# A fused transformer layer in fp32: four places where an in-order engine holds back TensorE are reordered or given buffers

## The chip, the cores and the metric

One Trainium2 chip, one of its cores. The metric is the time of one execution in device microseconds (us), without a profiler; three runs of the kernel before were timed. One further execution was taken with the hardware profiler, and all rows below come from it. Its time is compared with the runs in the section on the profile.

A core has TensorE (PE in the profile; PEld is its weight load), VectorE (DVE), ScalarE (ACT), GpSimd (POOL), and SyncE (SP), which here only issues transfers (DMA). Each of the engines works through one list of instructions in the order in which the program was built.

## The reference

One step of a small encoder layer for 1024 prompt rows and 8 x 16 sample rows (1152 rows, width 1024):

```
h   = RMSNorm(x)
z   = h @ W_in          # FoX q,k,v,logits | GDN q,k,v,a,b | GDN out gate gg | merge gates A,B
yA  = P_fox(FoX(h))     # causal attention with forget weights, 8 heads of 64
yB  = P_gdn(rmsnorm(GDN(h)) * silu(gg))   # gated delta rule, 8 heads of 64, chunks of 64 rows
x  += RMSNorm(W_out(sigmoid(gA) * yA + sigmoid(gB) * yB))
x  += RMSNorm(W_down relu(W_up RMSNorm(x))^2)      # 1024 -> 4096 -> 1024
```

It returns the new rows, and also FoX's keys and values, the logits, the GDN state and the last rows of the convolution. The GDN part solves one 64 x 64 triangular system for each chunk and head.

## The kernel before

All products are made in fp32 accuracy by splitting each operand into a high and a low part (`split`: a cast on ACT, L356, and a subtraction on DVE, L357) and adding three products (`mm3`, L157). Activations are kept transposed; a row block is `CH` = 384 columns, so that a product of 128 output features with 1152 rows is three chains of 24 matmuls, one for each `c`.

A scheduler of the framework orders the instructions of each engine at build time. It takes what is ready by its own estimate of durations, by priorities in the code: `tc.high_priority(n)` raises (or lowers) the priority of what stands under it, and `tc.issue_after(ins)` forbids it to be issued ahead of another instruction. On the chip the orders are fixed, and an engine whose next instruction isn't ready waits. A tile with `bufs=n` in a pool gets its memory in turn from n buffers under one tag; the next user waits until the last reader of that buffer is done, a DMA that stores it included.

The stages, with their place in the profiled execution:

- 0 to 50 us: RMSNorm of the rows, transposed by `to_T` (L195 casts the high part on ACT), and the first products. `early_parts` (L259) casts the weights of two small products.
- 50 to 660: the delta rule for four pairs of heads, p = 0 to 3. For each: `gdn_in` (products; ACT copies their banks to `X`, L428), `gdn_norms` (convolution on DVE, L478 to L482; Silu on ACT, L483), `gdn_systems` (decays: Exp on ACT, L543), `gdn_inverse` (30 steps of two DVE instructions, L592 and L593, a round trip through DRAM, a transposition, L609), `gdn_b` (states and outputs `oT`). At the end of `gdn_b` stands the gate: for each c, load `gg`, Silu on ACT (L702), two loads of row factors, a product on POOL (L704), and a product into `oT` on DVE (L705, "STT" below). The next pair's projections run beside it. The tiles `ro` and `gg` share three buffers of tag `be`.
- Into all of this, and into the next stage, the scheduler puts "fills": products of h with the weights for FoX, the out gate and the merge gates, at the lowest priority (`fill`, L407). They use two PSUM banks of tag `mf`; ACT copies each bank to a tile `gst` (L221) and sends it to DRAM (L222).
- 660 to 950: FoX. For a pair of heads `fox_prep` transposes v (two blocks of 512 columns and one of 128), then k alike. Each block is copied from its bank by ACT to a tile `kst` (L957, L969; v's last block goes to `vn`) and stored to the output by SP. `kst` has one buffer: every copy waits for the store ahead of it. For p = 1 to 3 this runs inside FoX, ahead of the pair that needs it.
- 950 to 1075: the merge: casts of `oparts` (`ohi<-orw`), Sigmoids of the gates `ga`, products, their sum. It may only start after the last fill (`issue_after(last_fill.ins)`). Then the output product, to 1200, and the up phase, to 1545.
- 1546 to 1895: the down phase, a fast matrix product of 7 passes `PASS = (1, 2, 3, 5, 6, 7, 4)`, each with 16 steps into four banks. The operands are split four steps ahead (`AHEAD`). At a pass's end `end(m, t, acc)` empties its four banks, for m = 2, 6 and 7 by additions on DVE (L1747 for m = 2). Six such banks and a bank for sums are there.

Of the kernel before, what the change touches and what calls it, by code (L numbers as in the profile page):

```python
# [72 lines left out]
def tile_step(ctx, tc, x_prompt, x_sample, cache_k, cache_v, cache_logf, state_gdn, state_conv,  # L73
# [140 lines left out]
    todo += [((W_MA, W_MB)[i] + j * P, gate_d[i, j]) for j in range(KT) for i in range(2)]  # L214

    def spill_out(pool, tag, bufs, w0, dst, c, acc):
        g = pool.tile([P, CH], F32, tag=tag, bufs=bufs, name=nm("gst"))
        if w0 < W_FK:
            A.activation(g, acc, AF.Copy, scale=-0.125)
        else:  # L220
            A.copy(g, acc)  # L221
        A.dma_start(dst[:, c * CH:(c + 1) * CH], g)  # L222
# [6 lines left out]
    with tc.tile_pool(name="p0", bufs=1) as p0:  # L229
# [60 lines left out]
        for t in range(NTT):  # L290
            xt = xts[t] if t < 6 else p0.tile([P, D], F32, tag="xt", bufs=6, name=nm("xt"))
            if t > 2:
                S.dma_start(xt, xp[t * P:(t + 1) * P] if t < 8 else xs)
            hns[t] = p0.tile([P, D], F32, tag="nh", name=nm("nh"), bufs=3)

            with tc.issue_after((nh if t < 3 else hh).ins) if t else ExitStack():
                nh = norm(xt, gb, p0, hns[t])
            if t == 0:
                raws = early_weights()
            if t == 2:  # L300
                with tc.issue_after(nh.ins):
                    logits_weights(raws)
                    for u in range(3):
                        if u == 2:
                            with tc.issue_after(hh.ins):
                                early_parts(raws)
                        hh = to_T(hns[u], u, hhi, hlo)
            elif t > 2:
                to_T(hns[t], t, hhi, hlo)
            if t % 3 == 2:  # L310
                logits_mm(t // 3)
                early_mm(t // 3)
            if t == 5:
# [94 lines left out]
    def fill():  # L408

        with tc.high_priority(-LOW):  # L410
            for w0, dst in todo[NE:]:
                mm = spill(w0, dst, "f", "mf", 20, MFB)
        return mm

# [98 lines left out]
    def gdn_systems(gp, p, qs, ks, vs, nv, kn, rows_n):  # L513
# [23 lines left out]
        d3 = u3(dk)  # L537
        G.tensor_tensor(d3, u3(gcb), bc(cols[:, 0], 2, [P, NU, C]), ALU.subtract)
        for u in (slice(0, NUP // 2), slice(NUP // 2, NUP)):
            V.tensor_tensor(d3[:, u], d3[:, u], bc(madd, 1, [P, NUP // 2, C]), ALU.add)  # L540
        V.tensor_tensor(d3[:, NUP:], d3[:, NUP:], bc(madds, 1, [P, NU - NUP, C]), ALU.add)
        A.activation(dk, dk, AF.Exp)
        A.activation(gcb, gcb, AF.Exp)  # L543
        gam = big(gp, "gam", 2, [P, NUP + NB])
# [38 lines left out]
        return kT, vs, qa, cols, gam, nv, kn, obd, sy  # L583

    def gdn_inverse(gp, obd, sy):


        st = big(gp, "st", 1, [4 * NU, 256])
        for k in range(1, 31):
            n = 31 - k  # L590
            tv = st[:, :k * n].rearrange("p (j i) -> p j i", j=k)
            V.tensor_tensor(tv, bc(sy[:, 0:k, k], 2, [4 * NU, k, n]), bc(sy[:, k, k + 1:], 1, [4 * NU, k, n]), ALU.mult)  # L592
            V.tensor_tensor(sy[:, 0:k, k + 1:], sy[:, 0:k, k + 1:], tv, ALU.subtract)  # L593
        V.memset(sy.rearrange("p j i -> p (j i)")[:, 0:1024:33], -1.0)
# [6 lines left out]
        for h in range(2):  # L601
# [5 lines left out]
            for q in range(2):  # L607
                S.dma_start(pk[r0:r0 + 64, q], inv_d[2 * h + q, 0:NUP].rearrange("(t u) j i -> (u j) t i", u=2))
        V.transpose(pk[:, 2].rearrange("p t i -> p (t i)"), pk[:, 0].rearrange("p t i -> p (t i)"))  # L609
        m2 = pt("pa", 1)  # L610
# [17 lines left out]
    def gdn_b(gp, p, kT, vs, qa, cols, gam, nv, kn, tt):  # L628
# [68 lines left out]
        to_rows(gp, nv[:, 1, :18], 18, rows_o.rearrange("h (t p) -> (h t) p", p=P), "pd", "rsbb")  # L697
        for c in range(3):
            cs = slice(c * CH, (c + 1) * CH)
            ro, gg = big(gp, "be", 3, [P, 512])[:, :CH], big(gp, "be", 3, [P, 512])[:, :CH]  # L700
            S.dma_start(gg, gg_d[p, :, cs])
            A.activation(gg, gg, AF.Silu)  # L702
            rows_bc(ro, rows_o[:, cs])
            G.tensor_tensor(gg, gg, ro, ALU.mult)  # L704
            V.scalar_tensor_tensor(oT[:, cs], oT[:, cs], ngc, gg, ALU.mult, ALU.mult)  # L705
        S.dma_start(gdn_d[p], oT)
        S.dma_start(gdn_p[0, 0, 2 * p:2 * p + 2].rearrange("h k v -> (h k) v"), st_)

    def to_rows(gp, src, n, dst, tag="pa", stag="rsb"):
# [232 lines left out]

    def fox_prep(fp, p, *banks):

# [3 lines left out]
        for src, i, dp, ds in ((v, 2, fv_p, fv_s), (k, 1, fk_p, fk_s)):  # L948
            S.dma_start(src, fr_d[i, p])
            for g in range(3):  # L950
                n = 4 if g < 2 else 1
                tp = banks[g % 2]() if banks else alt("pb", "pd")
                for j in range(n):
                    T.transpose(tp[:, j * P:(j + 1) * P], src[:, (4 * g + j) * P:(4 * g + j + 1) * P], ident)
                if g < 2:
                    st = fp.tile([P, 4, P], F32, tag="kst", bufs=1, name=nm("kst"))
                    A.copy(st.rearrange("p a n -> p (a n)"), tp)  # L957
                    S.dma_start(dp[0, 0, g * 512:(g + 1) * 512, 2 * p:2 * p + 2].rearrange(
                        "(a t) h d -> t a (h d)", a=4), st)
                    if src is v:  # L960
                        blk = v2[:, 4 * g:4 * g + 4].rearrange("p t (a d) -> p t a d", a=4)
                        sv = st.rearrange("p t (a d) -> p t a d", a=2)
                        A.copy(blk[:, :, 0:4:3], sv)
                        V.tensor_tensor(blk[:, :, 1:3], sv, f(blk[:, :, 0:4:3]), ALU.subtract)
                else:
                    st = vn
                    if src is k:
                        st = fp.tile([P, 4, P], F32, tag="kst", bufs=1, name=nm("kst"))[:, 0]
                    A.copy(st, tp[:, :P])  # L969
                    S.dma_start(ds[0][:, :, 2 * p:2 * p + 2].rearrange("b t h d -> (b t) (h d)"), st)  # L970
# [7 lines left out]
    with tc.tile_pool(name="gp", bufs=1, reuse_waits="tile") as gp:  # L978
# [6 lines left out]
        for kd in kds:  # L985
            G.memset(kd, 0.0)
        last_fill = fill()
        nxt = gdn_norms(gp, 0, *gdn_in(gp, 0, lg))
        cur = None
        for p in range(NG):  # L990
# [4 lines left out]
            with tc.high_priority(IOFF):  # L995
                tt = gdn_inverse(gp, *cur[7:])
            prev = *cur[:7], tt
            if p == 0:
# [16 lines left out]
            with tc.high_priority(BOFF):  # L1015
                gdn_b(gp, p, *prev)

# [135 lines left out]
    with tc.tile_pool(name="fp", bufs=1, reuse_waits="tile") as fp:  # L1153
# [17 lines left out]
        for p in range(NP_):  # L1171
            q, k, v2, vn, qkn = nxt
            oT = fp.tile([P, NPR], F32, tag="oT", bufs=2, name=nm("oT"))
            for hh in range(2):
# [12 lines left out]
                for s in (3, 2, 1, 0) if (p, hh) == (3, 1) else range(4):  # L1187
                    pr = fox_scores(fp, s, *qk)
                    if p + hh + s == 0:
                        first = tre[0]  # L1190
                    if late:
                        values(*late)
                    late = p, hh, s, pr, v2, oT
                    for sm in sms:
                        next(sm, None)
                    if hh and p < 3 and s == 1:
                        nxt = fox_prep(fpa, p + 1)
        values(*late)
# [34 lines left out]
    with tc.tile_pool(name="op", bufs=1, reuse_waits="tile") as op:  # L1233
# [28 lines left out]
        with tc.high_priority(200):  # L1262
# [6 lines left out]
            for c in (1, 0):  # L1269
                for k in range(4):  # L1270
                    load(1, k, c)
        def merge_weights(j):
# [3 lines left out]
        for j in range(KT):  # L1276
# [7 lines left out]
            for c, i in [(c, i) for i in (1, 0) for c in (2, 1, 0)] if j == 0 else [(c, i) for c in range(3) for i in (1, 0)]:  # L1284
# [5 lines left out]
                with tc.high_priority(200):  # L1290
                    if j == 0 and i:
                        ga = gas_[c]
                        with tc.issue_after(sp_.ins):
                            A.activation(ga, ga, AF.Sigmoid)
# [448 lines left out]
    def end(m, t, acc):  # L1743
        if m == 1:
            A.copy(yb[t][:, L], acc)
        elif m == 2:
            V.tensor_tensor(ya[t][:, L], acc, yb[t][:, L], ALU.add)  # L1747
        elif m == 3:
# [3 lines left out]
        elif m == 6:  # L1752
            V.tensor_tensor(yb[t][:, L], acc, yb[t][:, L], ALU.add)
            V.tensor_tensor(ya[t][:, R], ya[t][:, R], yb[t][:, R], ALU.add)
            V.tensor_tensor(ya[t][:, R], ya[t][:, R], yb[t][:, L], ALU.add)
        elif m == 7:
            V.tensor_tensor(yb[t][:, L], acc, yb[t][:, L], ALU.add)
            V.tensor_tensor(yb[t][:, R], yb[t][:, R], yb[t][:, L], ALU.add)
        else:
            y, (xt, ss) = yb[t], last[t]  # L1760
            with tc.high_priority(200):
# [9 lines left out]
                y_rows(xt, 4 + t, R)  # L1771

    def terms(hs, ls):

        return [(hs[0], ls[0]), (hs[0], ls[1]), (hs[1], ls[0])]

    for m in PASS:
# [59 lines left out]
```

## Time and profile before

| | |
|---|---|
| timed runs | 1892.69, 1892.87, 1893.63 us; median 1892.87 |
| profiled execution | 1903.8 us, span 1902.1 |
| PE busy | 1856.8 us, 98% of the span |
| DVE, ACT, POOL busy | 67%, 54%, 11% |

The profiled execution took 10.9 us more than the median. PE was idle for 1902.1 - 1856.8 = 45.3 us of its span; this counts only time in which no matmul ran, not time in which matmuls ran at a lower clock. A share of 98% says little on where time goes; the places where PE waited are in the view of waits, and the times at a lower clock in the windows, which have a granted clock for each stretch.

### The profile page before, as it was taken

The page shows a single profiled execution, that of the slowest core. Times are in us where ns is not written, and L with a number is a line of the kernel's source. Part 1 is how long each engine was busy: PE and PEld are TensorE (multiplying, and loading weights), DVE is VectorE, ACT ScalarE, POOL GpSimd, SP SyncE. Part 2 cuts the span into 40 slices and gives each one's busy share as a digit, 9 for nine tenths or more (in the row PEclk, how much of TensorE's full clock was granted, in tenths as well). Part 3 has the DMA queues.
Part 4 walks back from the last instruction along what each step waited for, and adds up shares of the span by engine and source line. Part 5 has one row for each costly group of instructions (what it writes and reads, how often), then busy time and mean ns, then how long its engine had stood idle before and what let it go on. Part 6 is the DMA issues. An engine that isn't in the chain of part 4 may idle for free. (4 is left out here: it accounts for less than half of the span.)

```text
span 1902.1 us, 31953 instructions
## 1 busy us (share of the span) xinstructions
PE 1856.8 (98%) x11035; PEld 1684.2 (89%) x11035; DVE 1270.7 (67%) x3096; ACT 1019.6 (54%) x2381; POOL 204.9 (11%) x340
## 2 busy tenths in 40 slices
PE   7999999999999999999999999999999999999998
PEld 6989989898898988888889988999999998788886
DVE  7458477686764385777555466977776664659697
ACT  6353574764847474666454454554555554345453
POOL 1221232322412100000012100000000000000000
PEclk9999999999999998999999999999999999999999
DMA  7133323233354353543355641244444478846473
GB/s 211 38 95 84 90 74 103 55 92 104 75 141 137 115 159 114 150 114 101 95 183 158 193 154 65 61 134 136 146 136 132 131 234 287 276 135 179 151 265 133
DMA packets 291155, 258.49 MB, mean 136 GB/s; under 512 B 68620, under 2 KB 245948, under 8 KB 290993
## 3 DMA queue, kind: packets, MB, share of 16 engines
q1 hardware_dynamic: 250629, 221.98, 39.7%
q10 hardware_dynamic: 40364, 34.47, 5.5%
q8 instruction: 87, 1.43, 0.3%
q14 instruction: 75, 0.61, 0.1%
HBM read 183.66 MB, written 72.71 MB: 135 GB/s over the span
## 5 line engine op out<-in xcount | busy, mean ns | idle before, releaser
L157 PE MATMUL mf<-hhi,whi 128*128 128x384 f32 x744 | 261.5, 351 | 2.5 <-ACT gst L221 2.4
L157 PE MATMUL mf<-hlo,whi 128*128 128x384 f32 x744 | 261.9, 352 | 0.0
L157 PE MATMUL mf<-hhi,wlo 128*128 128x384 f32 x744 | 261.6, 352 | 0.0
L157 PE MATMUL mm<-th,wh 128*128 128x320 f32 (+1 forms) x896 | 177.9, 295 | 0.0
L157 PE MATMUL mm<-bh,ah 128*128 128x512 f32 x436 | 169.7, 389 | 1.5 <-DVE y L1747 1.5
L157 PE MATMUL mm<-bl,ah 128*128 128x512 f32 x436 | 169.7, 389 | 0.0
L157 PE MATMUL mm<-bh,al 128*128 128x512 f32 x436 | 169.7, 389 | 0.0
L356 ACT CAST ah<-ar 128x512 fp32r<-128x512 f32 x107 | 66.4, 622 | 153.6 <-PE mm L157 101.6
L157 PEld LDWEIGHTS mf<-hhi,whi 128*128 128x128 f32 x744 | 141.0, 190 | 4.0 <-ACT gst L221 3.3
L157 PEld LDWEIGHTS mm<-th,wh 128*128 128x128 f32 x896 | 143.0, 188 | 0.0
L157 PEld LDWEIGHTS mf<-hhi,wlo 128*128 128x128 f32 x744 | 141.1, 190 | 0.7
L157 PEld LDWEIGHTS mf<-hlo,whi 128*128 128x128 f32 x744 | 141.0, 189 | 0.8
L157 PE MATMUL mm<-th,wl 128*128 128x256 f32 x448 | 131.4, 293 | 0.0
L1511 DVE TENSOR_TENSOR s<-mm,s 128x256 f32<-128x256 f32 (+1 forms) x196 | 84.3, 454 | 66.9 <-PE mm L157 53.8
L357 DVE TENSOR_TENSOR al<-ar,ah 128x512 fp32r<-128x512 f32 x107 | 73.7, 689 | 75.6 <-ACT ah L356 74.0
L357 DVE TENSOR_TENSOR wlo<-raw,whi 128x512 fp32r<-128x512 f32 x110 | 80.1, 730 | 49.0 <-ACT whi L356 43.9
L157 PE MATMUL mm<-hhi,whi 128*128 128x384 f32 x288 | 105.6, 367 | 4.3 <-ACT X L428 4.2
L356 ACT CAST whi<-raw 128x512 fp32r<-128x512 f32 x110 | 67.8, 619 | 70.1 <-PE mm L157 32.8
L157 PE MATMUL mm<-hhi,wlo 128*128 128x384 f32 x288 | 99.5, 346 | 0.0
L157 PE MATMUL mm<-hlo,whi 128*128 128x384 f32 x288 | 99.2, 345 | 0.0
L157 PE MATMUL mm<-mhi,wh 128*128 128x256 f32 (+1 forms) x336 | 99.1, 295 | 0.0
L157 PE MATMUL mm<-mlo,wh 128*128 128x256 f32 (+1 forms) x336 | 98.9, 294 | 0.0
(550 smaller groups left out, 4914.9 us busy)
## 6 DMA issues: line engine op xcount, KB each, us to landing
ar<-ua_d SPq DMA_DIRECT2D x124, 256.0 KB
raw<-in_w_in_dram SPq DMA_DIRECT2D x86, 256.0 KB
br<-in_w_down_dram SPq DMA_DIRECT2D x78, 256.0 KB
wr<-in_w_up_dram SPq DMA_DIRECT2D x56, 256.0 KB
ua_d<-s SPq DMA_DIRECT2D x112, 128.0 KB
ua_d<-s ACTq DMA_DIRECT2D x84, 128.0 KB
gate_d<-gst ACTq DMA_DIRECT2D x48, 192.0 KB
ga<-gate_d SPq DMA_DIRECT2D x48, 192.0 KB
```

The costliest lines, as they stand in the source:

```text
L157: mm = T.matmul(out, a, b, start=first and i == 0, stop=last and i == n - 1)
L356: a = A.copy(h, raw)
L357: V.tensor_tensor(l, raw, f(h), ALU.subtract)
L1511: V.tensor_tensor(r, o, x, ALU.add)
```

## The change

It has five parts. No matmul is added or taken away.

1. **Start.** The casts of `early_parts` come behind all three `to_T`, and no longer between the second and the third.
2. **Gates.** `gdn_b` returns the gate as a function; it is called after `gdn_inverse` of the next pair, and its three products on DVE may be issued only behind that inverse's steps 24, 28 and its transposition (called 31). The last pair's gate stays where it was. In `gdn_systems` a subtraction on POOL (1152 columns) is cut in two, and two Exp on ACT in two halves each: 4 instructions more on POOL and 8 on ACT.
3. **Keys and values.** Where `fox_prep` runs inside FoX (p = 1 to 3), `kst` has three buffers.
4. **Merge.** The splits of the GDN operands for c = 1 and 0 may be issued only behind the copies of the third-last and the second-last bank of the fills, the first three Sigmoids only behind the last copy. Before, these Sigmoids were issued after the splits for c = 2.
5. **Down phase.** In the last step of a pass the operands of a coming step are made after the banks are emptied (for m = 2, 6, 7 behind the last addition), and the second additions for m = 6 and 7 follow after all four first ones.

```diff
@@ spill_out
-            A.copy(g, acc)
+            gsts.append(A.copy(g, acc))
@@ start
                     for u in range(3):
-                        if u == 2:
-                            with tc.issue_after(hh.ins):
-                                early_parts(raws)
                         hh = to_T(hns[u], u, hhi, hlo)
+                    with tc.issue_after(hh.ins):
+                        early_parts(raws)
@@ fill
-        return mm
+        return mm, gsts[-3:]
@@ gdn_systems
-        G.tensor_tensor(d3, u3(gcb), bc(cols[:, 0], 2, [P, NU, C]), ALU.subtract)
+        for u in (slice(0, NUP // 2), slice(NUP // 2, NU)):
+            G.tensor_tensor(d3[:, u], u3(gcb)[:, u], bc(cols[:, 0, u], 2, [P, u.stop - u.start, C]), ALU.subtract)
...
-        A.activation(dk, dk, AF.Exp)
-        A.activation(gcb, gcb, AF.Exp)
+        for x in (dk, gcb):
+            for c in HALF:
+                A.activation(x[:, c], x[:, c], AF.Exp)
@@ gdn_inverse
-            V.tensor_tensor(sy[:, 0:k, k + 1:], sy[:, 0:k, k + 1:], tv, ALU.subtract)
+            steps[k] = V.tensor_tensor(sy[:, 0:k, k + 1:], sy[:, 0:k, k + 1:], tv, ALU.subtract)
...
-        V.transpose(pk[:, 2]...)
+        steps[31] = V.transpose(pk[:, 2]...)
@@ gdn_b (the loop over c is unchanged but for the issue_after)
+        def gate(behind=()):
+            for c in range(3):
...
+                with tc.issue_after(behind[c].ins) if behind else ExitStack():
+                    V.scalar_tensor_tensor(oT[:, cs], oT[:, cs], ngc, gg, ALU.mult, ALU.mult)
+            S.dma_start(gdn_d[p], oT)
...
+        return gate
@@ the loop over pairs, after gdn_inverse
+            if p:
+                with tc.high_priority(BOFF):
+                    gate([steps[k] for k in (24, 28, 31)])
...
-                gdn_b(gp, p, *prev)
+                gate = gdn_b(gp, p, *prev)
+                if p == NG - 1:
+                    gate()
@@ FoX
-                        nxt = fox_prep(fpa, p + 1)
+                        nxt = fox_prep(fpa, p + 1, kst=lambda _: fp.tile([P, 4, P], F32, tag="kst", bufs=3, name=nm("kst")))
@@ merge
             for c in (1, 0):
-                for k in range(4):
-                    load(1, k, c)
+                with tc.issue_after(last_gst[1 - c].ins):
+                    for k in range(4):
+                        load(1, k, c)
...
-                        with tc.issue_after(sp_.ins):
+                        with tc.issue_after(last_gst[2].ins):
                             A.activation(ga, ga, AF.Sigmoid)
@@ down phase, end
         elif m == 6:
-            V.tensor_tensor(yb[t][:, L], acc, yb[t][:, L], ALU.add)
-            V.tensor_tensor(ya[t][:, R], ya[t][:, R], yb[t][:, R], ALU.add)
-            V.tensor_tensor(ya[t][:, R], ya[t][:, R], yb[t][:, L], ALU.add)
+            return V.tensor_tensor(yb[t][:, L], acc, yb[t][:, L], ALU.add)
@@ down phase, the loop over passes
-            nx = next(made, None)
-            if nx is not None:
-                ahead.append(nx)
+            if pr < NPAIR - 1:
+                more()
...
-            end(m, t, acc[t])
+            e = end(m, t, acc[t])
+        with tc.issue_after(e.ins) if m in (2, 6, 7) else ExitStack():
+            more()
+        for t in range(4):
+            after(m, t)       # the second additions of m = 6 and 7
```

The change also moves what the scheduler decides. In the order of PE, the fill matmuls that stand between the first FoX scores and the start of the merge are as many as before, but 72 of them have left the places between FoX's own products: the run of nothing but fills ahead of the merge has 185 matmuls, and had 113.

Three places show what moves. The first is ACT in FoX, where `fox_prep` for p = 1 copies its blocks. `kst<-pd` with 128x512 is a half of v or of k, and `kst<-pb` with 128x128 is k's last block; `sp` are scores, `phi` the casts of weights, `gst` a fill. Before (both halves of v and the first half of k stand further up, 18, 12 and 7 rows ahead of the second half of k):

```order
L1068 ACTIVATE sp_9116,m_9117<-sp_9116,m_9117 128x128
L1068 ACTIVATE sp_9126,m_9127<-sp_9126,m_9127 128x256
L1038 CAST yk_9419<-kz_8534 64x1024
L957 COPY kst_8945<-pd_8940 128x512
L222 DMA gate_d<-gst_2852 128x384
L221 COPY gst_2880<-mf_2855 128x384
L1090 CAST phi_8991<-pd_8986 128x512
L222 DMA gate_d<-gst_2880 128x384
L356 CAST whi_3009<-raw_3007 128x512
L969 COPY kst_8950<-pb_8948 128x128
```

The same place now, from the first half of v to the last block of k:

```order
L970 COPY kst_8924<-pd_8919 128x512
L976 CAST v_1550_8916<-kst_8924 128x4x2x64
L1150 ACTIVATE prs_8907,m_8908<-prs_8907,m_8908 128x384
L970 COPY kst_8934<-pb_8929 128x512
L982 COPY vn_8917<-pd_8939 128x128
L976 CAST v_1550_8916<-kst_8934 128x4x2x64
L1087 ACTIVATE sp_8969,m_8970<-sp_8969,m_8970 128x640
L970 COPY kst_8949<-pb_8944 128x512
L970 COPY kst_8957<-pd_8952 128x512
L1087 ACTIVATE sp_8983,m_8984<-sp_8983,m_8984 128x768
L982 COPY kst_8962<-pb_8960 128x128
```

The five copies stand within 11 rows. With three buffers the second half of k (`kst_8957`) takes the buffer of v's first half (`kst_8924`), and k's last block that of v's second half.

The second place is ACT where pair 1's projection for k runs beside the gate of pair 0. `be` are the Silu of the gate, `ks` the Silu of the convolution's result, `X` copies of a projection's bank, `y` squares for the norm. Before:

```order
L702 ACT_TABLE_LOAD
L702 ACTIVATE be_5382<-be_5382 128x384
L222 DMA fr_d<-gst_1276 128x384
L483 ACTIVATE ks_5619<-ks_5619 128x1152
L702 ACTIVATE be_5390<-be_5390 128x384
L428 COPY X_5633<-mm_5648 128x384
L490 ACTIVATE y_5705<-ks_5619 128x1152
L221 COPY gst_1316<-mf_1291 128x384
L222 DMA gg_d<-gst_1316 128x384
L428 COPY X_5633<-mm_5674 128x384
```

Now:

```order
L484 ACT_TABLE_LOAD
L484 ACTIVATE ks_5600<-ks_5600 128x1152
L429 COPY X_5614<-mm_5629 128x384
L491 ACTIVATE y_5686<-ks_5600 128x1152
L710 ACTIVATE be_5870<-be_5870 128x384
L223 COPY gst_1316<-mf_1291 128x384
L224 DMA gg_d<-gst_1316 128x384
L710 ACTIVATE be_5878<-be_5878 128x384
L429 COPY X_5614<-mm_5655 128x384
```

The first copy of `X` no longer has two Silu of the gate ahead of it; the second copy has both.

The third place is DVE at the end of pass 2 of the down phase. `y<-mm` empties a bank; `wb` are operands of pass 5, `al`, `bl` and `sl` the low parts of the next steps' operands. Before:

```order
L1661 TENSOR_TENSOR wb_18159<-br_19884,wb_18159 128x512
L1661 TENSOR_TENSOR wb_18160<-br_19922,wb_18160 128x512
L357 TENSOR_TENSOR al_19417<-ar_19410,ah_19416 128x2x4x64
L357 TENSOR_TENSOR bl_19421<-wb_18177,bh_19420 128x512
L357 TENSOR_TENSOR sl_19457<-sr_19446,sh_19456 128x128
L1747 TENSOR_TENSOR y_18299<-mm_18846,y_18303 128x512
L1747 TENSOR_TENSOR y_18300<-mm_18847,y_18304 128x512
L1747 TENSOR_TENSOR y_18301<-mm_18848,y_18305 128x512
L1747 TENSOR_TENSOR y_18302<-mm_18849,y_18306 128x512
L357 TENSOR_TENSOR al_19449<-ar_19443,ah_19448 128x2x4x64
```

Now:

```order
L1682 TENSOR_TENSOR wb_18170<-br_19858,wb_18170 128x512
L1682 TENSOR_TENSOR wb_18171<-br_19896,wb_18171 128x512
L1682 TENSOR_TENSOR wb_18172<-br_19953,wb_18172 128x512
L1768 TENSOR_TENSOR y_18311<-mm_18858,y_18315 128x512
L1768 TENSOR_TENSOR y_18312<-mm_18859,y_18316 128x512
L1768 TENSOR_TENSOR y_18313<-mm_18860,y_18317 128x512
L1768 TENSOR_TENSOR y_18314<-mm_18861,y_18318 128x512
L358 TENSOR_TENSOR al_19406<-ar_19400,ah_19405 128x2x4x64
L358 TENSOR_TENSOR al_19429<-ar_19422,ah_19428 128x2x4x64
```

The fourth `wb` still stands ahead of the additions, but `al`, `bl` and `sl` of one step have gone behind them.

More of the change, by code (lines that the diff above doesn't have):

```diff
@@ L214, in tile_step @@
     todo += [((W_MA, W_MB)[i] + j * P, gate_d[i, j]) for j in range(KT) for i in range(2)]
+    gsts = []
     def spill_out(pool, tag, bufs, w0, dst, c, acc):
@@ L583, in gdn_systems @@
         return kT, vs, qa, cols, gam, nv, kn, obd, sy
+    steps = {}
     def gdn_inverse(gp, obd, sy):
@@ L608, in gdn_inverse @@
                 S.dma_start(pk[r0:r0 + 64, q], inv_d[2 * h + q, 0:NUP].rearrange("(t u) j i -> (u j) t i", u=2))
-        V.transpose(pk[:, 2].rearrange("p t i -> p (t i)"), pk[:, 0].rearrange("p t i -> p (t i)"))
+        steps[31] = V.transpose(pk[:, 2].rearrange("p t i -> p (t i)"), pk[:, 0].rearrange("p t i -> p (t i)"))
         m2 = pt("pa", 1)
@@ L697, in gdn_b @@
         to_rows(gp, nv[:, 1, :18], 18, rows_o.rearrange("h (t p) -> (h t) p", p=P), "pd", "rsbb")
[L698 to L706, printed above, removed]
+        def gate(behind=()):
+            for c in range(3):
+                cs = slice(c * CH, (c + 1) * CH)
+                ro, gg = big(gp, "be", 3, [P, 512])[:, :CH], big(gp, "be", 3, [P, 512])[:, :CH]
+                S.dma_start(gg, gg_d[p, :, cs])
+                A.activation(gg, gg, AF.Silu)
+                rows_bc(ro, rows_o[:, cs])
+                G.tensor_tensor(gg, gg, ro, ALU.mult)
+                with tc.issue_after(behind[c].ins) if behind else ExitStack():
+                    V.scalar_tensor_tensor(oT[:, cs], oT[:, cs], ngc, gg, ALU.mult, ALU.mult)
+            S.dma_start(gdn_d[p], oT)
         S.dma_start(gdn_p[0, 0, 2 * p:2 * p + 2].rearrange("h k v -> (h k) v"), st_)
+        return gate
     def to_rows(gp, src, n, dst, tag="pa", stag="rsb"):
@@ L941, in fox_rows, with kst, fox_prep @@
         return nfb
-    def fox_prep(fp, p, *banks):
+    def kst(fp):
+        return fp.tile([P, 4, P], F32, tag="kst", bufs=1, name=nm("kst"))
+    def fox_prep(fp, p, *banks, kst=kst):
         v, k, q = (fp.tile([P, NT], F32, tag=x, bufs=1, name=nm(x)) for x in ("qv", "kr", "qv"))
@@ L955, in fox_prep @@
                 if g < 2:
-                    st = fp.tile([P, 4, P], F32, tag="kst", bufs=1, name=nm("kst"))
+                    st = kst(fp)
                     A.copy(st.rearrange("p a n -> p (a n)"), tp)
@@ L967, in fox_prep @@
                     if src is k:
-                        st = fp.tile([P, 4, P], F32, tag="kst", bufs=1, name=nm("kst"))[:, 0]
+                        st = kst(fp)[:, 0]
                     A.copy(st, tp[:, :P])
@@ L986, in tile_step @@
             G.memset(kd, 0.0)
-        last_fill = fill()
+        last_fill, last_gst = fill()
         nxt = gdn_norms(gp, 0, *gdn_in(gp, 0, lg))
@@ L1746, in end @@
         elif m == 2:
-            V.tensor_tensor(ya[t][:, L], acc, yb[t][:, L], ALU.add)
+            return V.tensor_tensor(ya[t][:, L], acc, yb[t][:, L], ALU.add)
         elif m == 3:
@@ L1752, in end @@
         elif m == 6:
-            V.tensor_tensor(yb[t][:, L], acc, yb[t][:, L], ALU.add)
-            V.tensor_tensor(ya[t][:, R], ya[t][:, R], yb[t][:, R], ALU.add)
-            V.tensor_tensor(ya[t][:, R], ya[t][:, R], yb[t][:, L], ALU.add)
+            return V.tensor_tensor(yb[t][:, L], acc, yb[t][:, L], ALU.add)
         elif m == 7:
-            V.tensor_tensor(yb[t][:, L], acc, yb[t][:, L], ALU.add)
-            V.tensor_tensor(yb[t][:, R], yb[t][:, R], yb[t][:, L], ALU.add)
+            return V.tensor_tensor(yb[t][:, L], acc, yb[t][:, L], ALU.add)
         else:
@@ L1771, in end, with after, more @@
                 y_rows(xt, 4 + t, R)
+    def after(m, t):
+        if m == 6:
+            V.tensor_tensor(ya[t][:, R], ya[t][:, R], yb[t][:, R], ALU.add)
+            V.tensor_tensor(ya[t][:, R], ya[t][:, R], yb[t][:, L], ALU.add)
+        elif m == 7:
+            V.tensor_tensor(yb[t][:, R], yb[t][:, R], yb[t][:, L], ALU.add)
     def terms(hs, ls):
         return [(hs[0], ls[0]), (hs[0], ls[1]), (hs[1], ls[0])]
+    def more():
+        nx = next(made, None)
+        if nx is not None:
+            ahead.append(nx)
     for m in PASS:
```

## The prediction

> **What bounds the kernel now.** I read the page first, for the engines and the clock, then the view of waits for PE, then the windows around the largest waits, then the timelines of ACT, DVE, POOL and SP there.
>
> ```profile
> span 1902.1 us, 31953 instructions
> PE 1856.8 (98%) x11035; PEld 1684.2 (89%) x11035; DVE 1270.7 (67%) x3096; ACT 1019.6 (54%) x2381; POOL 204.9 (11%) x340
> ```
>
> PE is the bound, and the change leaves its matmuls alone. So it can win only the time in which PE stands, 45.3 us, and the time in which it runs at a lower clock. The waits that the change aims at:
>
> ```profile
> engine line waited for: us in total, times, longest us
> ...
> PE mm L157 <- ACT X L428: 4.2, 3, 2.4
> ...
> PE pb L1086 <- ACT kst L969: 2.6, 1, 2.6
> PE mf L157 <- ACT gst L221: 2.4, 1, 2.4
> ...
> PE mm L157 <- DVE y L1747: 1.5, 1, 1.5
> ```
>
> Together 10.7 us of 45.3. Each is PE waiting for an engine that works through its list in order and had something else in front. The clock comes on top:
>
> ```profile
> core 0: us, PE busy (x) PEld busy (x) DVE busy (x) ACT busy (x) POOL busy (x), PEclk, DMA share, GB/s
> ...
> 310.00:315.00 5.00, 5.00 (x22) 5.00 (x21) 4.76 (x11) 0.34 (x2) 2.70 (x4) 0.67 0.65 192
> ...
> 720.00:725.00 5.00, 2.36 (x13) 2.07 (x11) 1.51 (x5) 1.78 (x6) 0.00 (x0) 0.79 0.68 238
> 725.00:730.00 5.00, 5.00 (x24) 4.91 (x25) 1.75 (x7) 0.70 (x3) 0.00 (x0) 0.50 0.17 50
> 730.00:735.00 5.00, 5.00 (x24) 4.82 (x24) 2.24 (x4) 2.44 (x5) 0.00 (x0) 0.69 0.28 69
> ```
>
> The PEclk column tells of the granted clock. After the wait for `kst` it is 0.79, 0.50 and 0.69 over three windows of 5 us: 5 x (0.21 + 0.50 + 0.31) = 5.1 us of work lost while PE reads as busy. After the longest wait for `X` it is 0.67, 5 x 0.33 = 1.7 us. After the wait for `gst`, of 2.4 us too, the clock stayed full. So the lower clock follows some waits and not others.
>
> **Keys and values.** What holds ACT there:
>
> ```profile
> 716.08 0.57 ACT L957 COPY kst<-pd 128x512 f32<-128x512 f32 x1
> ...
> 718.18 0.62 ACT L356 CAST whi<-raw 128x512 fp32r<-128x512 f32 x1
> 722.61 0.27 ACT L969 COPY kst<-pb 128x128 f32<-128x128 f32 x1 [3.81 <-DMA out_dram<-kst]
> ```
> ```profile
> 716.68 0.39 SPq L958 DMA_DIRECT2D out_dram<-kst  x1
> ```
>
> The copy ends at 716.65, the store is issued at once, and the next copy into the same buffer starts at 722.61: a store holds the buffer for 6.0 us. ACT stands for 3.81 of these with the copy at its head; behind it wait casts that PE needs. With three buffers k's last block waits for a store five copies and casts further back, and this wait goes: -2.6, and the clock behind it, -5.1 if it goes too. What can be late next is the second half of k, which now takes the buffer of v's first half. Seven instructions stand between the two in ACT's new order: four copies and casts of 512 columns at about 0.6 us by the rows above (0.57, 0.62), one Exp over 384 and one over 640 columns, which I put at 0.6 and 0.8, and a copy of 128 at 0.27. That makes 4.1 us, against 6.0 for the store. If ACT ran without a gap it would stand 1.9 us, three times over (p = 1 to 3), 5.7 at most. It runs at 54% over the span and waits for PE's transposes here, so the gap is mostly filled; nothing at the other end. I take 1.0 in all.
>
> **The filler in FoX.** 72 fill matmuls leave FoX for the run ahead of the merge. A window within the run of fills before:
>
> ```profile
> 963.00:968.00 5.00, 5.00 (x30) 5.00 (x29) 1.52 (x3) 1.41 (x3) 0.00 (x0) 1.00 0.61 184
> ```
>
> 30 matmuls in 5.00 us are 0.17 us each, so 72 are 12.2 us of cover. Without the `kst` row, what PE waited between 660 and 950 (the view of waits, cut to this stretch) is
>
> ```profile
> PE pc L1095 <- ACT phi L1090: 1.4, 2, 0.8
> PE pc L1095 <- DVE plo L1091: 0.6, 2, 0.3
> ```
> ```profile
> L157 PE MATMUL mf<-hlo,whi x194: 332/338/522, 659.8 to 949.7; 128*128 128x384 f32 x194
> ```
>
> and a few tenths. This row and its two like it make some 580 fills in FoX, so one in eight leaves. If all the cover that goes had been needed the cost is 12.2; if it stood in front of waits that go as well, as around `kst`, nothing. The waits that are left are nearest to this end, so I take a doubling of the waits that are there: +2.0. The fills themselves cost the same wherever they stand.
>
> **Gates.** The rows around the longest wait for `X` (PE stands until the copy at 308.18 ends) and around the second:
>
> ```profile
> 303.80 0.62 DVE L705 SCALAR_TENSOR_TENSOR oT<-oT,ngc,be 128x384 f32<-128x384 f32 x1 [3.73 <-POOL be L704]
> ```
> ```profile
> 307.75 0.52 ACT L702 ACTIVATE be<-be 128x384 f32<-128x384 f32 x1 [0.22 <-DMA be<-gg_d]
> 308.18 0.46 ACT L428 COPY X<-mm 128x384 f32<-128x384 f32 x1
> ...
> 429.90 0.53 ACT L702 ACTIVATE be<-be 128x384 f32<-128x384 f32 x1 [4.37 <-DMA be<-gg_d]
> ...
> 434.26 0.46 ACT L428 COPY X<-mm 128x384 f32<-128x384 f32 x1
> 434.62 1.17 ACT L490 ACTIVATE y<-ks 128x1152 f32<-128x1152 f32 x1
> 439.32 0.48 ACT L428 COPY X<-mm 128x384 f32<-128x384 f32 x1 [3.53 <-PE mm L157]
> ```
> ```profile
> 426.84 0.53 SPq L701 DMA_DIRECT2D be<-gg_d  x1
> ```
> ```profile
> 429.54 1.01 POOL L704 TENSOR_TENSOR be<-be,be 128x384 f32<-128x384 f32 x1 [3.90 <-DMA be<-rows_o]
> ```
>
> DVE stood 3.73 us with the gate's product at its head, the convolution behind it was late by that, the Silu of `ks` on ACT too, and the copy of `X` stands behind all of them. The change puts the gate's products behind late steps of the inverse and the Silu of `ks` and the first copy of `X` ahead of the gate's Silu. All three waits for `X` go: -4.2, and the clock after the first, -1.7 if it goes too. The second copy now has both Silu ahead of it, and the last of them needs a load that may start only when POOL's product ahead is done. From the end of the first Silu that is 1.01 for POOL and 429.90 - 426.84 = 3.06 for the load. Counted from the start of the first copy: 0.46 + 1.17 + 0.53 + 1.01 + 3.06 + 0.53 = 6.8 us until the second can start, and in the rows above it started after 5.06, when PE's bank was ready. So it may be 1.7 late, at p = 1, and PE has other work for part of it; at most 3.5 for two pairs, at best nothing. I take 1.0. The products on DVE hold up the inverse only if POOL is late; they are issued when the inverse has few and short steps left. The transfer of `oT` follows its last product, behind the transposition, and that is far from the next writer. The 12 instructions more on POOL and ACT: engines at 11% and 54%, nothing.
>
> **Merge.**
>
> ```profile
> 956.43 1.89 ACT L356 CAST ohi<-orw 128x384 fp32r<-128x384 f32 x4
> ...
> 959.47 0.47 ACT L221 COPY gst<-mf 128x384 f32<-128x384 f32 x1
> ```
>
> The copy of a fill's bank stands behind casts and Sigmoids for the merge. With the casts behind the last copies, the wait goes: -2.4. The casts of 0.5 us each then stand between the copies, four at a time, 1.9 us, less than the 24 x 0.17 = 4.1 us that PE takes for a bank. What is late next is the first gating on DVE, which needs three Sigmoids to have followed the last copy; it needs a chain of 12 matmuls too, 2.0 us, and each Sigmoid is one more cast's length, 1.5 in all. Nothing.
>
> **Down phase and start.**
>
> ```profile
> 1654.32 0.69 DVE L1661 TENSOR_TENSOR wb<-br,wb 128x512 f32<-128x512 f32 x1 [1.53 <-DMA br<-in_w_down_dram]
> 1654.93 0.69 DVE L357 TENSOR_TENSOR al<-ar,ah 128x512 fp32r<-128x512 f32 x1
> ...
> 1656.34 2.48 DVE L1747 TENSOR_TENSOR y<-mm,y 128x512 f32<-128x512 f32 x4
> ```
>
> The additions stand behind `wb`, which waited for its transfer, and `al`, `bl`, `sl` of one step. These three go behind; `wb` stays. The additions start at 1654.93 at the earliest: -1.4. The operands that go behind are for a step three ahead; 7 x 16 steps between 1546 and 1895 make 3.1 us a step, so they have 9. The additions for passes 6 and 7 have no wait in the view; nothing. At the start two casts leave the way of the last `to_T`:
>
> ```profile
> 15.44 1.99 PE L157 MATMUL pa<-hhi,wl 128*64 128x384 f32 x8 [0.29 <-ACT hhi L195]
> ```
>
> -0.3.
>
> **The sum.** Waits removed: 2.6 + 4.2 + 2.4 + 1.4 + 0.3 = 10.9. Lower clock removed: between 0 and 5.1 + 1.7 = 6.8. I take half, 3.4, because one wait of 2.4 us in this trace was followed by it and one was not. New waits: 1.0 + 2.0 + 1.0 = 4.0. Net -10.3 against the profiled 1903.8, which gives 1893.5, 0.54% less. The same share of the median of the runs, 1892.87, gives 1882.6.
>
> **Rivals.**
>
> *The clock is not the waits'.* The lower clock stays or falls elsewhere: -10.9 + 4.0 = -6.9, 1886.0. For it: the clock after 960 stayed full. [...]
>
> *Everything goes and nothing comes:* the whole clock, no new waits, -17.7, 1875.3. For it: ACT and DVE have room on average. Against it: each part leaves something on an engine in order.
>
> *The waits only move.* The second half of k stands 1.9 us in each of three pairs, 5.7; the second copy of `X` is late by 3.5; FoX waits 2.0 more: 11.2 against 10.9 and no clock: 1893, the same. For it: a store held its buffer for 6.0 us, and the new order leaves 4.1.
>
> *Slower.* FoX needed the 72 fills. Then its chains (scores on PE, Exp on ACT, cast, PE again) show as waits of 12.2 us, and if one of them is long enough a stretch at half clock like the one at 725 follows, 5.1. With 2.0 for the other new waits that is 19.3, against 14.3 that go: +5.0, 1898. It decides from 12.3 us of new waits in FoX. Against it: those fills stood in part in front of waits that go, and the waits left now are 2 us in 290.
>
> **Chances.** Forecast 0.42, clock not the waits' 0.18, everything 0.12, waits only move 0.15, slower 0.13. About 0.2%, 3.8 us, is what a measurement of this kernel can tell from no change. The first three are faster by more: 0.72; the fourth is within: 0.15; the last slower: 0.13. The range of 8 in 10 reaches from the third, 1875, to the fourth, 1893. The forecast's own is 1879 to 1888.
>
> **What would show it.** In the profile after, the waits for `kst` L969's successor, `gst`, `y` and `X` are gone from the top of PE's waits, and the windows of 5 us between 700 and 740 have a granted clock of 1.00. If ACT idles ahead of a `kst` copy for a store, with PE waiting for ACT then, the price of the stores was wrong; if PE's waits in FoX beyond those rise over 4 us, the filler's was. DVE should not idle for POOL inside the inverse. If the profiled span falls by 14 and the runs only by 6, the clock was a matter of the profiled execution. The prediction is wrong above all if FoX takes longer than its 290 us less the 12.2 of fills that have left it.

## The result, and the profile after

The changed kernel took 1883.55 us (median of 6 runs, 1878.30 to 1886.60), the kernel before 1893.11 beside it. The ratio is 0.9942, with a 95% interval of 0.9922 to 0.9962: faster by 0.6%. The forecast was 1882.6. The total came out; several of its terms did not, and two large errors cancel: keys and values won some 8 us more than forecast, and the clock some 4.5 less.

Each run comes with its span and its mean granted clock, and a single run of the changed kernel is 1878.3 at a clock of 0.999 or 1886.6 at 0.996. So two numbers stand beside each median from here on. *Lost to the clock* is span x (1 - clock); *at full clock* is the time less that. The clock has three decimals, so each run is known to about 1 us, and means are given over all runs with their standard error. The profiles of both kernels end at half clock behind PE's last matmul, for 5.0 us of the span before and 5.2 after, where it costs nothing; a run at 0.999 (1.9 us "lost") has little besides. With the rounding it can have lost 2.8 at most, so, whatever its tail, no more than one stretch of 3.41 us at half clock, the shortest in the profile before, which costs 1.7, can be hidden in it.

| kernel | runs | median | at full clock | lost to the clock, mean (range) |
|---|---|---|---|---|
| before | 67 | 1894.65 | 1889.9 +- 0.2 | 4.9 (1.9 to 9.5) |
| changed | 11 | 1885.09 | 1877.8 +- 0.4 | 6.0 (1.9 to 9.4) |

The 67 are the runs of the kernel before that stood beside the experiments; the six beside the first result have no clock on record, and the profiled execution of 1903.8 us is not counted. Differences here and below are taken before rounding. At full clock the change wins 12.2 us; at the clock it wins nothing (+1.1 +- 0.9).

The page of the changed kernel's profile, which caught an execution without half clock:

```profile
span 1876.8 us, 31969 instructions
PE 1842.5 (98%) x11035; PEld 1674.7 (89%) x11035; DVE 1275.3 (68%) x3096; ACT 1017.4 (54%) x2389; POOL 208.4 (11%) x344
PEclk9999999999999999999999999999999999999999
```

This span is 25.3 us below the one before, far more than the medians differ: the profile before lost 8.5 us to stretches at half clock (3.41, 3.41 and 10.24 us long), this one none, and that is the luck of two executions. What PE waited for, in the changed kernel:

```profile
engine line waited for: us in total, times, longest us
...
PE mm L157 <- ACT X L429: 2.9, 2, 2.2
...
PE mf L157 <- ACT gst L223: 0.7, 1, 0.7
PE pc L1114 <- ACT phi L1109: 0.7, 1, 0.7
...
PE pb L1105 <- ACT kst L982: 0.4, 1, 0.4
PE mm L157 <- DVE y L1768: 0.4, 1, 0.4
```

`kst` went from 2.6 to 0.4 and `y` from 1.5 to 0.4. The wait for `gst` ahead of the merge, 2.4, is gone: the 0.7 in the view is another one, in the delta rule. `X` only went from 4.2 to 2.9, and has one long wait of 2.2 us until 432.6; the kernel before waited 1.5 us near there, for an earlier copy.

### The profile page after: what moved, and what is told of

It reads as the page before. It is cut to its first block, busy times and chain, and to the rows that moved or that the text cites. A ratio compares the mean times of both kernels' runs of the same rounds, so it can differ in the third digit from the quotient of the medians.

```text
span 1876.8 us, 31969 instructions
## 1 busy us (share of the span) xinstructions
PE 1842.5 (98%) x11035; PEld 1674.7 (89%) x11035; DVE 1275.3 (68%) x3096; ACT 1017.4 (54%) x2389; POOL 208.4 (11%) x344
## 4 chain that ended last, share of the span: by engine, by line
PE 87%; ACT 4%; DVE 3%; DMA 3%; issue 1%; POOL 1%; SPq 0%; DVEq 0%; ACTq 0%; POOLq 0%
PE mm L157 49%; PE mf L157 18%; PE pc L1114 2%; PE pa L157 1%; PE pb L157 1%; PE pc L157 1%; PE pd L157 1%; PE pe L157 1%; PE pc L689 1%; PE pd L1105 1%; PE pa L563 1%; PE pb L1105 1%; PE mm L1164 1%; PE mm L1143 1%; PE pd L698 1%
## 5 line engine op out<-in xcount | busy, mean ns | idle before, releaser
L157 PE MATMUL mm<-mhi,wl 128*128 128x256 f32 (+1 forms) x336 | 98.8, 294 | 0.0
```

The source lines that it names most:

```text
L157: mm = T.matmul(out, a, b, start=first and i == 0, stop=last and i == n - 1)
```

## The experiments

### Four parts, each alone on the kernel before

**Keys and values** (`only_kst`):

```diff
-                        nxt = fox_prep(fpa, p + 1)
+                        nxt = fox_prep(fpa, p + 1, kst=lambda _: fp.tile([P, 4, P], F32, tag="kst", bufs=3, ...))
```

> The kernel before with part 3 alone: three buffers for the stored keys and values inside FoX; 72 fills leave FoX with it. Theory A (removed waits and the PE time around them): FoX from its first scores to the last fill becomes shorter by 8 to 12 us in the profile, of which 2.6 are the wait and up to 5.1 lower clock, and the runs' median falls by 5 to 8 us. Rival B (the prediction's terms): 2.6 less 3.0 of new waits and half the clock, so the median falls by only 0 to 3 us. Rival C (the 72 fills were needed): the median rises, and PE's waits in FoX without the stores exceed 4 us.

**Gates** (`only_gates`): `gate()` returned and called behind the next inverse, with the pieces of Exp and subtraction.

> The kernel before with part 2 alone: gates behind the next pair's inverse, subtraction and Exp in pieces. Theory A (the prediction's terms): the waits for X before 450 us go (4.2), the second copy is late by about 1 us, the median falls by 2 to 5 us, and FoX, merge and down phase keep their length. Rival B (the waits only move to copies of the states and to the second copy of X): within 1.5 us of before.

**Merge** (`only_merge`):

```diff
             for c in (1, 0):
+                with tc.issue_after(last_gst[1 - c].ins):
                 ...
-                        with tc.issue_after(sp_.ins):
+                        with tc.issue_after(last_gst[2].ins):
```

> The kernel before with part 4 alone: the merge's splits and Sigmoids behind the copies of the last fills. Theory A: the wait for a fill's copy (2.4 us) goes or falls under 1, the merge starts no later after the last fill than before, the median falls by 1.5 to 2.5 us. Rival B: the merge's first products wait for the splits that were held back: the median is within 1 us of before.

**Down phase** (`only_down`): `more()` behind the additions in a pass's last step, second additions in `after()`.

> The kernel before with part 5 alone: banks emptied first at the end of a pass. Theory A: the wait of 1.5 us at the end of pass 2 falls to some tenths, and the median falls by 1.0 to 1.5 us. Rival B: the operands made later are missed in the next pass, and nothing is won (within 0.7 us).

| part alone | runs | median | ratio to before | at full clock | against before there | lost to the clock |
|---|---|---|---|---|---|---|
| kst | 5 | 1884.07 | 0.9946 [0.9934, 0.9959] | 1881.7 +- 0.6 | -8.3 | 2.6 |
| gates | 12 | 1898.03 | 1.0008 [0.9993, 1.0024] | 1886.9 +- 0.4 | -3.1 | 10.0 |
| merge | 12 | 1890.60 | 0.9984 [0.9974, 0.9995] | 1886.9 +- 0.4 | -3.1 | 4.3 |
| down | 11 | 1893.34 | 0.9990 [0.9980, 0.9999] | 1888.5 +- 0.3 | -1.4 | 4.6 |

Keys and values carry over half of it: theory A, and the median fell by more than it said, 10.5. The run of fills ahead of the merge has 185 matmuls in this kernel too, so it is this part that moves the 72 fills, and PE's waits in FoX did not grow where they left. What PE waited for between 660 and 970 us, in `only_kst`:

```profile
PE pc L1100 <- ACT phi L1095: 0.9, 1, 0.9
PE pb L1091 <- ACT kst L974: 0.5, 1, 0.5
...
PE mf L157 <- ACT gst L223: 0.4, 1, 0.4
```

and in `only_down`, which leaves this stage as before:

```profile
PE mf L157 <- ACT gst L223: 2.3, 1, 2.3
PE pc L1097 <- ACT phi L1092: 1.4, 2, 0.8
PE pb L1088 <- ACT kst L971: 1.3, 1, 1.3
```

From FoX's first values to the last fill PE stood 3.1 us in the first and 7.4 in the second, and the stretches are 282.6 and 291.4 us long. The wait for a fill's copy goes with part 3 as with part 4, so on this wait, of some 2 us, the two parts overlap. Of the 8.8, 4.3 are idle time and 1.7 half clock in the second; some 2.8 more lie in the spacing of matmuls that both count as busy, and what these are stays open. The buffers and the 72 fills came together in every run, so how much each of them is worth stays open too.

Merge and down phase are theory A as well, the merge with somewhat more than the wait of 2.4. The gates have theory A's number at full clock (-3.1), but not the rest of it: the waits for `X` did not go (3.5 us are left of 4.2, and the longest is 2.3), and the median rose by 3.4 where a fall of 2 to 5 was expected. 10.0 us are lost to the clock on average, against 4.9. Windows of `only_gates` show one such execution:

```profile
core 0: us, PE busy (x) PEld busy (x) DVE busy (x) ACT busy (x) POOL busy (x), PEclk, DMA share, GB/s
430.00:435.00 5.00, 2.69 (x11) 2.36 (x11) 4.31 (x10) 1.27 (x3) 2.37 (x3) 0.83 0.62 168
435.00:440.00 5.00, 5.00 (x20) 5.00 (x20) 1.26 (x2) 0.00 (x0) 1.43 (x4) 0.50 0.54 90
440.00:445.00 5.00, 5.00 (x20) 5.00 (x19) 0.79 (x2) 1.42 (x3) 0.93 (x3) 0.50 0.20 34
445.00:450.00 5.00, 5.00 (x25) 5.00 (x24) 4.67 (x12) 2.10 (x5) 0.61 (x2) 0.81 0.01 1
```

PE stood 2.3 us until 432.8 for `X`, and by these clocks it ran at half clock from 433.3 for 13.6 us: 5 x (0.17 + 0.50 + 0.50 + 0.19) / 0.5. In the changed kernel the same wait of 2.2 us stands at the same place, followed in the profiled execution by the full clock:

```profile
430.00:435.00 5.00, 2.81 (x19) 2.50 (x18) 4.57 (x11) 1.27 (x3) 2.38 (x5) 1.00 0.57 166
435.00:440.00 5.00, 5.00 (x34) 5.00 (x34) 2.23 (x6) 1.37 (x3) 1.54 (x5) 1.00 0.56 95
```

### What the wait for X at 432 us is

ACT, SP and POOL of the changed kernel around it:

```profile
423.22 0.53 ACT L710 ACTIVATE be<-be 128x384 f32<-128x384 f32 x1
423.65 1.15 ACT L484 ACTIVATE ks<-ks 128x1152 f32<-128x1152 f32 x1
424.70 0.46 ACT L429 COPY X<-mm 128x384 f32<-128x384 f32 x1
...
431.62 0.52 ACT L710 ACTIVATE be<-be 128x384 f32<-128x384 f32 x1 [5.39 <-DMA be<-gg_d]
432.05 0.46 ACT L429 COPY X<-mm 128x384 f32<-128x384 f32 x1
```
```profile
429.18 0.34 SPq L709 DMA_DIRECT2D be<-gg_d  x1
```
```profile
428.11 1.05 POOL L712 TENSOR_TENSOR be<-be,be 128x384 f32<-128x384 f32 x1 [3.41 <-DMA be<-rows_o]
```

POOL's product of the second block waited 3.41 us for its row factors and ended at 429.16; the load of the third block's `gg`, into a buffer which that product freed, was issued at 429.18; the Silu on it started at 431.62, with ACT standing 5.39 us; the second copy of `X` stood behind it. By the program these are the copies for v of pair 2 (the index `i` is 2 in the edit below), and not for k of pair 1, as the text on the change has it. The experiment exchanges just these last two on ACT (`late_silu`):

```diff
+                    z = A.copy(x[:, 3 + c * CH:3 + (c + 1) * CH], acc)
+                    if (c, i) == (1, 2):
+                        xk.append(z)
...
+                with tc.issue_after(xk[-1].ins) if behind and c == 2 else ExitStack():
                     A.activation(gg, gg, AF.Silu)
```

> The changed kernel with one pair of instructions exchanged on ACT, twice (for pairs 0 and 1): the second copy of X now stands ahead of the gate's last Silu, not behind it. Theory A (the Silu waits for a load that may only start behind POOL's product, and the copy of X behind it): PE's wait for X of 2.2 us near 432 us goes or falls under 1, and at full clock the time is 1.5 to 2.5 us below that of the changed kernel, with fewer stretches at half clock. Rival B (the copy is late because PE's bank is late, or the next copy takes the wait): no difference, within 1 us.

```profile
422.94 0.46 ACT L431 COPY X<-mm 128x384 f32<-128x384 f32 x1
423.29 1.17 ACT L495 ACTIVATE y<-ks 128x1152 f32<-128x1152 f32 x1
427.94 0.48 ACT L431 COPY X<-mm 128x384 f32<-128x384 f32 x1 [3.48 <-PE mm L157]
430.39 0.52 ACT L715 ACTIVATE be<-be 128x384 f32<-128x384 f32 x1 [1.96 <-DMA be<-rows_o]
```

The copy now starts when PE's bank is ready, 5.0 us after the first, and `X` is gone from PE's waits. The five runs took 1875.89 to 1877.73, median 1877.14, ratio 0.9910 [0.9894, 0.9925]: the fastest of all kernels here. At full clock that is 1875.2 +- 0.3, 2.6 below the changed kernel, and **all five ran at 0.999**. Another 4.1 us are the clock: the changed kernel loses 6.0 on average, this one 1.9. PE works through the same matmuls in the same order in both. No gap of PE in its profile is over 1.1 us behind the start.

The changed kernel once more (`after_again`), to see whether the clock explains its spread:

> The changed kernel itself once more, beside the others of this call. Theory A (waits of over 1 us in the delta rule bring on stretches at half clock in some executions and not in others): the time at full clock stays at 1876 to 1879, the single runs spread over 5 us or more, and the loss to the clock explains the spread. Rival B (the spread has another cause): the runs differ at the same granted clock.

Median 1885.41 (1881.73 to 1887.96), ratio 0.9953 [0.9941, 0.9966]; from the fastest to the slowest the five runs had a clock of 0.999, 0.996, 0.997, 0.995 and 0.995, and at full clock 1878.1 +- 0.8. Theory A holds for most of the spread. A part of rival B is left: the two runs at 0.995 differ by 2.2 us, and the three at 0.999 of both sets by 3.4, where the rounding of the clock allows 1.9.

### Parts taken from the changed kernel

Without part 2 (`less_gates`), without part 3 (`less_kst`), and without the pieces of part 2 alone (`less_pieces`):

> The changed kernel without part 2: the gate at the end of gdn_b as before, subtraction and Exp whole. Theory A (the parts add): at full clock 2 to 3 us slower than the changed kernel, since part 2 alone took 2 to 3 us there, and the runs' median differs by less than 2 because its stretches at half clock go too. Rival B (part 2 costs what it wins by its new wait for X): at full clock within 1 us.

> The changed kernel without part 3: one buffer for stored keys and values. Theory A (the parts add): 7 to 9 us slower than the changed kernel at full clock, with the store's wait and a run of 113 fills ahead of the merge. Rival B (part 4 or 2 had taken some of it already, the wait for a fill's copy above all, which is gone with part 3 as with part 4): 4 to 6 us slower.

> The changed kernel with the subtraction and the Exp whole, as before; the gates stay moved. Theory A (the pieces are off the path): within 1 us of the changed kernel at full clock. Rival B (the pieces let the copies of the states through ACT, and are part of what the gates' part won): 1.5 us or more slower at full clock.

| changed kernel without | median | ratio to before | at full clock | against changed (1877.8) | lost to the clock |
|---|---|---|---|---|---|
| part 2 (6 runs) | 1885.22 | 0.9952 [0.9935, 0.9969] | 1883.0 +- 0.6 | +5.2 | 2.2 |
| part 3 (12) | 1895.57 | 0.9995 [0.9980, 1.0010] | 1885.6 +- 0.6 | +7.8 | 8.7 |
| the pieces (11) | 1892.60 | 0.9986 [0.9972, 1.0000] | 1884.9 +- 0.5 | +7.1 | 6.0 |

Part 3 is worth as much on top as alone. Without part 2 the median is that of the changed kernel: 5.2 us slower at full clock, 3.8 less lost to the clock. The surprise is the pieces: with the gates moved but Exp and subtraction whole, 7.1 us are lost, theory B. So moving the gates alone is worth nothing in this kernel (1884.9 without the pieces, 1883.0 without both), and the pieces make part 2; the pieces without the moved gates were not run. Windows of the delta rule, first of `after_again`, then of `less_pieces`:

```profile
200.00:330.00 130.00, 127.48 (x807) 120.44 (x805) 94.89 (x286) 81.11 (x224) 41.89 (x58) 1.00 0.35 92
```
```profile
200.00:330.00 130.00, 124.63 (x781) 116.10 (x780) 92.98 (x284) 80.72 (x220) 36.94 (x57) 1.00 0.33 85
```

PE stands 2.9 us more there and starts 26 matmuls fewer. One wait shows what the pieces do. In `less_pieces` PE waits for the state `S`, which DVE makes:

```profile
PE pb L669 <- DVE S L682: 1.2, 1, 1.2
...
PE pd L669 <- DVE S L682: 0.8, 1, 0.8
```
```profile
219.72 2.12 POOL L539 TENSOR_TENSOR y<-gcb,cols 128x1152 f32<-128x1152 f32 x1
```
```profile
221.87 1.20 DVE L541 TENSOR_TENSOR y<-y,madd 128x512 f32<-128x512 f32 x1 [1.16 <-POOL y L539]
223.00 0.27 DVE L682 SCALAR_TENSOR_TENSOR S<-S,gam,pd 128x64 f32<-128x64 f32 x1
```

POOL's whole subtraction takes 2.12 us; DVE stands 1.16 for it, with an addition at its head that needs its result, and `S` stands behind that addition. All six profiles without part 2, the one before among them, have 2.3 us of this wait, `less_pieces` 2.0, and those with the pieces none. That is some 2 of the 7.1 us. The scheduler also orders the stage anew (9 fills more go ahead of FoX), and over the whole profile PE stands 36.6 us here against 34.3 and 35.3 in the two of the changed kernel; so in these executions most of the 7.1 is not standing, and what it is stays open, as does the share of the halved Exp.

### Two buffers instead of three

`kst_two` is the changed kernel with `bufs=2` in part 3.

> The changed kernel with two buffers for stored keys and values instead of three. 63 fills leave FoX, against 72 with three. Theory A (FoX gains by fewer fills between its products): nearly the whole gain stays, within 1.5 us of the changed kernel at full clock, even if ACT stands for a store now and then. Rival B (the gain is the wait for the stores): a store holds its buffer for some 6 us, ACT stands in front of k's copies in each pair, PE waits 2 us or more there, and 3 us or more are lost.

Median 1885.47, ratio 0.9954 [0.9938, 0.9970]; at full clock 1880.1 +- 0.5, 2.3 slower. It lies between: 63 of the 72 fills have left FoX, ACT stood 2.1 us for stores, and of part 3's 7.8 us some 5.5 stay. Neither theory alone.

### The start

`only_start` is part 1 alone.

> The kernel before with part 1 alone: the casts of two small products behind all three transpositions. Theory A (the prediction's term): 0.3 us, which cannot be told from nothing here (within 1.5 us at full clock). Rival B (the small products' operands come late): 1.5 us or more slower.

Median 1895.11, ratio 1.0003 [0.9994, 1.0011], at full clock 1890.7 +- 0.4: no difference.

## Why the prediction was right, and where it was not

Against the terms of its sum, in us:

| step | forecast | measured |
|---|---|---|
| keys and values, filler: -2.6 + 1.0 + 2.0 | +0.4 | -8.3 alone, -7.8 in the whole |
| gates: -4.2 + 1.0, pieces 0 | -3.2 | -3.1 alone, -5.2 in the whole; pieces -7.1 |
| merge | -2.4 | -3.1 (+- 0.5) alone |
| down phase | -1.4 | -1.4 (+- 0.4) alone |
| start | -0.3 | +0.7 (+- 0.4) alone |
| at full clock | -6.9 | -12.2 (+- 0.5) |
| clock | -3.4 | +1.1 (+- 0.9) |
| sum | -10.3 | -11.0 (means of all runs) |

The parts do not add: alone they come to -15.1 at full clock (+- 1.4), together to -12.2.

**Merge and down phase** were right in place and size: one wait each, a copy or an addition behind work that nobody needed yet. In the changed kernel DVE at the end of pass 2:

```profile
1631.02 0.69 DVE L1682 TENSOR_TENSOR wb<-br,wb 128x512 f32<-128x512 f32 x1 [2.69 <-DMA br<-in_w_down_dram]
1631.63 2.48 DVE L1768 TENSOR_TENSOR y<-mm,y 128x512 f32<-128x512 f32 x4
```

The additions follow `wb` directly; `wb` still waits for its transfer, which is the 0.4 that is left.

**Keys and values**: the steps that failed are the two new waits. The store was priced at 6.0 us and ACT's way between two users of a buffer at 4.1:

```profile
694.53 0.58 ACT L970 COPY kst<-pd 128x512 f32<-128x512 f32 x1 [0.76 <-PE pd L967]
...
699.64 0.59 ACT L970 COPY kst<-pd 128x512 f32<-128x512 f32 x1 [0.29 <-DMA out_dram<-kst]
701.05 0.26 ACT L982 COPY kst<-pb 128x128 f32<-128x128 f32 x1
```

The store held the buffer until 699.6, 4.5 us past the copy's end, and ACT stood 0.29. The term for lost filler, +2.0, did not come either: PE stood 3.1 us in this stage with the fills gone, and 7.4 with them. A reading of this, which no run tests, is that the scheduler had put fills where it saw waits, and that they left with the waits. Beyond that the part also took the wait for a fill's copy and some 2.8 us of matmul spacing, which the view of waits does not list. The wait that was to go is not a constant either: it was 2.6 in the profile before, and 1.3 and 1.2 in `only_down` and `only_merge`, whose FoX is the same.

**Gates**: -3.1 alone against -3.2 is luck, for the term was made of waits for `X`, and these did not go. The six profiles with the old gates have 2.7 to 4.2 us of them (4.2, 3.1, 3.3, 2.7, 2.7, 3.6), the five with part 2 whole 2.9 to 3.9 (3.5, 2.9, 3.3, 3.1, 3.9): near 432 us, what the first copy gained the second lost. The wait that did go is the one for `S`, 2.3 us, which the forecast did not list and which is the pieces' work. The mechanism of the new wait was right; its size was not. From the first copy to the second 6.8 us were added up, and it was 7.35: POOL's product waited 3.41 us for its row factors, a load that the sum had left out, and the load of `gg` was shorter than assumed. PE then waited 2.2 and 2.6 us in the two profiles, where 1.7 was worked out and 1.0 taken, because PE was thought to have other work. DVE's standing for POOL fell as forecast, from

```profile
L705 DVE SCALAR_TENSOR_TENSOR oT<-oT,ngc,be 128x384 f32<-128x384 f32 x12 | 8.3, 692 | 22.8 <-POOL be L704 22.8
```

to

```profile
L714 DVE SCALAR_TENSOR_TENSOR oT<-oT,ngc,be 128x384 f32<-128x384 f32 x12 | 7.7, 644 | 6.5 <-POOL be L712 6.5
```

The 12 small instructions were costed at nothing because POOL is busy for 11% and ACT for 54%. That is the plainest error: the share of busy time says nothing on a chain in which the next engine waits for one long instruction, as DVE did for POOL's 2.12 us.

**The clock**: half of the half-clock time of the one profile was taken as won. None was, in sum. By parts it was: with three buffers the mean loss falls, from 4.9 to 2.6 alone and from 8.7 to 6.0 in the whole; with the moved gates it rises, from 4.9 to 10.0 alone and from 2.2 to 6.0 in the whole. The rival "the clock is not the waits'" is wrong in its reason, though: `late_silu` took the waits for `X` away and the loss fell from 6.0 on average to 1.9 in every run. The forecast did not count that a new wait can be followed by half clock, as the one of 2.3 us in `only_gates` was, by 13.6 us. A wait's length does not settle the matter: those of 2.2 and 2.6 us in the two profiles of the changed kernel had a clock of 1.00 behind them. The profile before had 8.5 us of it, where its runs lose 4.9 - 1.9 = 3.0 on average beyond the tail, so the term was also read from an unlucky execution.

## What to carry to other kernels

Where a loaded buffer is freed by another engine's product, the consumer of that load is late by the whole chain (product, issue, landing; ACT stood 5.39 us here); on an in-order engine put what TensorE waits for ahead of it. Take the clock from many runs, not from the profiled one, and count a wait of TensorE at its own length, and allow for some us at half clock behind it in a part of the executions: here it was 3.4 to 13.6 us, behind waits of 0.8 to 2.6 us. Do not cost an instruction by its engine's share of busy time: ask who waits for its end.

## What the runs showed of the hardware

Half clock came in stretches, and behind short waits. The profile before has three that PE worked in, by windows of 0.2 us: 3.41 us from 224.5, 2.1 us after a wait of 1.16 for `S` ended; 3.41 us from 309.8, 1.2 us after the wait of 2.42 for `X`; and 10.24 us, three times 3.41, from 722.9, as the wait of 2.64 for `kst` ended. Around the first:

```profile
222.36 0.43 PE L666 MATMUL pb<-S,kbdb 128*128 128x64 f32 x2 [1.16 <-DVE S L679]
```
```profile
220.00:225.00 5.00, 3.84 (x23) 3.23 (x23) 3.44 (x8) 4.54 (x11) 1.57 (x2) 0.95 0.06 18
225.00:230.00 5.00, 5.00 (x27) 4.94 (x27) 2.91 (x11) 3.92 (x11) 2.40 (x3) 0.71 0.00 0
```

`only_gates` had 13.6 us from 433.3, 0.5 us behind a wait of 2.3. Waits like these in other executions had no such effect: the two profiles of the changed kernel waited 2.2 and 2.6 us for `X`, and the clock is 1.00 in every window of the delta rule. `late_silu`, whose longest waits behind the start are 1.0 us, ran five times at 0.999, which leaves room for one stretch of 3.41 us each at most. But a wait under a microsecond had one behind it too: in `only_start` 5 x (0.30 + 0.04) / 0.5 = 3.4 us began at 722.0, and the only wait in the view between 690 and 725 us is one of 0.8, over by 720:

```profile
PE pb L1087 <- ACT kst L970: 0.8, 1, 0.8
```
```profile
715.00:720.00 5.00, 4.21 (x30) 3.75 (x29) 2.33 (x6) 2.25 (x6) 0.00 (x0) 1.00 0.96 310
720.00:725.00 5.00, 5.00 (x32) 4.91 (x32) 3.01 (x12) 1.92 (x6) 0.00 (x0) 0.70 0.66 207
725.00:730.00 5.00, 4.85 (x33) 4.56 (x33) 2.41 (x4) 2.53 (x6) 0.00 (x0) 0.96 0.35 100
```

At a granted clock of 1.00 the same matmuls of the up phase ran at two rates. The first row is of the changed kernel's first profile, the second of its other one:

```profile
1250.00:1450.00 200.00, 200.00 (x1520) 200.00 (x1520) 141.11 (x299) 102.32 (x227) 0.00 (x0) 1.00 0.45 138
```
```profile
1250.00:1450.00 200.00, 200.00 (x1515) 200.00 (x1514) 140.79 (x298) 101.83 (x225) 0.00 (x0) 1.00 0.45 137
```

That is 0.33% by the count, in profiles of one program. The kernel before and `only_gates` have 1515 in this window too, at 1.00. The 1518 matmuls that the first starts in this window took 200.0 us there and 200.8 in the profile before. No view shows a cause.
